# Seven of eleven pairs of the first SwiGLU products by seven products, with a pair's weights by quarters through the shared rings

## The chip, the cores and the metric

The kernel runs on one core of one Trainium2 chip. The metric is device time in microseconds (us) of one execution; before the change the median of three runs is 2079.83 us (2079.77 to 2080.1). Engines are named as in the profile: PE (TensorE matmul; PEld are its weight loads), DVE (VectorE), ACT (ScalarE), POOL (GpSimd), SP (SyncE, which issues most loads).

## The reference, cut to what matters

Two layers; each is a half-step SwiGLU, a mixer, and a second half-step SwiGLU, each followed by a residual sum and a layer norm. `x` is 512 positions by 1024 features, all in float32; `D_FF` is 2816, so `w13` is 1024 by 5632.

```python
def swiglu(x, w13, w2):
    a, b = jnp.split(x @ w13, 2, axis=-1)
    return (jax.nn.silu(a) * b) @ w2

for l in range(DEPTH):
    x = layer_norm(ALPHA * x + 0.5 * swiglu(x, ffn1_w13[l], ffn1_w2[l]), ln_g[l, 0], ln_b[l, 0])
    m = mixer(x, ...)
    x = layer_norm(ALPHA * x + m, ln_g[l, 1], ln_b[l, 1])
    x = layer_norm(ALPHA * x + 0.5 * swiglu(x, ffn2_w13[l], ffn2_w2[l]), ln_g[l, 2], ln_b[l, 2])
```

So there are four SwiGLU stages in a run, and the change is in the first product (`x @ w13`, then `silu(a) * b`) of each.

## The kernel before

Every float32 product is made of three products of `float32r` parts: an operand is split into a high part (ACT copies it with rounding, `split`, L119) and a low part (DVE subtracts, L122), and hi*hi, hi*lo and lo*hi are summed in PSUM. A split of a 128x1024 weight tile is one ACT and one DVE instruction.

The 5632 columns of `w13` are 22 blocks of 128 columns for `a` and 22 for `b`. Block k and block k+11 form a pair, k = 0 to 10. `ffn` works on the pairs in this order:

- `front`, pairs 8, 9, 10, the plain way: `plain` loads two weight blocks (`weights`, L124 to L133), makes 2 x 24 matmuls of 512 columns per block (`proj`, L147) and ends with `glu`. Beside them DVE and ACT form the sums of `x` that the other way needs (`x_sums`).
- `by_seven`, pairs 0 to 5 (`S_PAIRS` is 6): the 2 x 2 block product (features halved, positions halved; weight rows halved, `a` and `b` columns) by a Winograd form with seven products instead of eight. `seven_pair` issues seven products of 24 matmuls of 256 columns into four PSUM banks A, B, C, E (L548), and ACT and DVE take them out (L557 to L572).
- `behind`, pairs 6 and 7, the plain way again, while DVE forms the sums of the activations for the second product (`activation_sums`, L314 to L341), for all pairs from 10 and 0 onward.
- Then `Seven.run`, the second product (L363).

For one pair `weights_of_pair` loads four quarters of its weights (each 128 partitions x 2 blocks x 512), forms three further sums on DVE, and splits seven operands. Names before: `r_p` (two tiles, each an `a` quarter of the upper rows beside a `b` quarter of the lower rows), `rc` (`a`, lower rows), `rd` (`b`, upper rows); the sums are `t13` (two tiles, L521), `t2` (L522) and `rc + t2` (L526).

Buffers: a ring `raw` of 4 tiles for loaded weights (`NRAW`), a ring `w` of 10 tiles for split parts (`NW`, five operands of hi and lo), a ring `rs` of 2, a ring `sa` of 3, and 33 slots (`NS`) for everything that lives longer. Before, a pair takes two of `raw` (`r_p`), both of `rs` (`rc`, `rd`) and three slots (`t13` twice, `t2`); the first pair's `rc` and `rd` lie in slots and are loaded early (`raw_cd(..., True)`). A loaded tile's next use waits until its last reader is through: the load on SP waits for that instruction, and the queue of SP waits behind it.

Who sets the order: the code is written in the order above, and a scheduler of the framework moves instructions of an engine past each other by its own estimates when the program is built; what stands on an engine after that is fixed and runs in order. Beside the stage POOL issues DMAs that add up weight sums of the second product in DRAM (`sums_in_dram`, L288), a chain in which each step waits for the one before.

Of the kernel before, what the change touches and what calls it, by code (L numbers as in the profile page):

```python
# [35 lines left out]
P = 128  # L36
# [47 lines left out]
def trunk(ctx: ExitStack, tc, x_in, xt_in, w13, w2, w_in, w_br, w_out, ln_g, ln_b, lb_in, hgn, sgg, sgb, sgws,  # L84
# [18 lines left out]
    def slot(name, dtype=F32):  # L103
        return big.tile([P, 2, 512], dtype, tag="h", name=name, bufs=NS)
# [382 lines left out]
            s[c] = hi, lo  # L487
        return s

    def raw_cd(w13_of, k, early=False):  # L490

        if early:
            rc, rd = slot(f"rc{k}"), slot(f"rd{k}")
        else:
            rc, rd = (wk.tile([P, 2, 512], F32, tag="rs", name=f"r{c}{k}", bufs=2) for c in "cd")
        for z, j in enumerate((k, k + NH2)):
            nc.sync.dma_start(rd[:, z], w13_of(NF + j)[:, H[0]])
            nc.sync.dma_start(rc[:, z], w13_of(j)[:, H[1]])
        return rc, rd

    def weights_of_pair(w13_of, k, rcd=None):

        js = (k, k + NH2)
        ra = [wk.tile([P, 2, 512], F32, tag="raw", name=f"r_p{j}", bufs=NRAW) for j in js]
        rc, rd = rcd or raw_cd(w13_of, k)
        t13 = [slot(f"t13{j}") for j in js]
        t2 = slot(f"t2{k}")
        for z, j in enumerate(js):
            wa, wb = w13_of(j), w13_of(NF + j)
            nc.sync.dma_start(ra[z][:, 0], wa[:, H[0]])  # L510
            nc.sync.dma_start(ra[z][:, 1], wb[:, H[1]])

        def parts(raw, name, early=False):
            hi, lo = ((slot(f"{v}_{name}", F32R) if early else
                       wk.tile([P, 2, 512], F32R, tag="w", name=f"{v}_{name}", bufs=NW)) for v in "hl")
            split(hi, lo, raw, early)
            return [(hi[:, z], lo[:, z]) for z in range(2)]

        p = [parts(ra[z], f"p{j}") for z, j in enumerate(js)]
        for z in range(2):  # L520
            V.tensor_tensor(t13[z], ra[z], rd[:, z:z + 1].broadcast_to([P, 2, 512]), op=ALU.add)  # L521
            V.tensor_tensor(t2[:, z], ra[z][:, 0], t13[z][:, 1], op=ALU.add)  # L522
        w2 = parts(t2, f"t2{k}")
        wt = [parts(t13[z], f"t{j}") for z, j in enumerate(js)]
        w21 = parts(rc, f"c{k}", True)
        V.tensor_tensor(rc, rc, t2, op=ALU.add)  # L526
        w4 = parts(rc, f"d{k}", True)
        return p, wt, w2, w21, w4

    def seven_pair(seven, s, k, w):  # L530

        p, wt, w2, w21, w4 = w
        half = slice(0, 256), slice(256, 512)
        movs = {"A11": lambda m: (xh[m // 2][:, m % 2, half[0]], xl[m // 2][:, m % 2, half[0]]),
                "A12": lambda m: (xh[2 + m // 2][:, m % 2, half[0]], xl[2 + m // 2][:, m % 2, half[0]]),
                "A22": lambda m: (xh[2 + m // 2][:, m % 2, half[1]], xl[2 + m // 2][:, m % 2, half[1]])}
        for c in s:
            movs[c] = lambda m, c=c: (s[c][0][:, m], s[c][1][:, m])

        def product(ps, units, c, first=True):  # L540
            for z in range(2):
                hi, lo = units[z]
                for m in range(4):
                    ms = slice(m * P, (m + 1) * P)
                    mh, ml = movs[c](m)
                    for i, (a, v) in enumerate(((hi, mh), (hi, ml), (lo, mh))):
                        start = first and z == 0 and m == 0 and i == 0
                        PE.matmul(ps[:, half[z]], a[:, ms], v, start=start, stop=(m == 3 and i == 2),  # L548
                                  skip_group_check=not (first and z == 0))
                    flow.tick(3 * 120.0)  # L550

        A, B, C, E = (bank(f"f{c}{k}") for c in "ABCE")
        r = seven.room(k).rearrange("p q t -> p (q t)")
        lower, upper = r[:, 0:512], r[:, 512:1024]
        b0, b1 = (wk.tile([P, T], F32, tag="sa", name=f"b{c}", bufs=NSA) for c in "01")
        product(A, [p[0][0], p[1][0]], "A11")
        S.activation(upper, A, AF.Copy)  # L557
        product(B, w2, "s2")
        V.tensor_tensor(upper, upper, B, op=ALU.subtract)
        product(C, [wt[0][0], wt[1][0]], "s1")  # L560
        V.tensor_tensor(b1, C, upper, op=ALU.subtract)
        product(E, [wt[0][1], wt[1][1]], "s3")
        V.tensor_tensor(b1, b1, E, op=ALU.subtract)
        product(A, w21, "A12", False)
        S.activation(lower, A, AF.Silu)
        product(C, [p[0][1], p[1][1]], "s4", False)
        V.tensor_tensor(b0, C, upper, op=ALU.subtract)
        V.tensor_tensor(lower, lower, b0, op=ALU.mult)
        product(E, w4, "A22", False)
        V.tensor_tensor(upper, E, upper, op=ALU.add)  # L570
        S.activation(upper, upper, AF.Silu)
        V.tensor_tensor(upper, upper, b1, op=ALU.mult)  # L572

    S_PAIRS = 6

    def ffn(l, i, last=False, first_of_all=False):
        seven = Seven(lambda k: w2[l, i, k])
        w13_of = lambda j: w13[l, i, j]

        def blocks(j, early=False):  # L580
            return (weights(w13_of(j), f"a{j}", early), weights(w13_of(NF + j), f"b{j}", early),
                    bank(f"pa{j}"), bank(f"pb{j}"))

        def pair_of(j, args, n0, n):
            wa, wb, pa, pb = args
            proj(pa, wa, 0, from_x, KT, n0, n)
            proj(pb, wb, 0, from_x, KT, n0, n)

        def glu(j, args):
            wa, wb, pa, pb = args  # L590
            k, a = j % NH2, j // NH2
            sa = wk.tile([P, T], F32, tag="sa", name="sa", bufs=NSA)
            S.activation(sa, pa, AF.Silu)
            V.tensor_tensor(seven.part(k, a), sa.rearrange("p (h t) -> p h t", h=2),
                            pb.rearrange("p (h t) -> p h t", h=2), op=ALU.mult)

        front = list(range(Seven.KEPT, NH2))
        by_seven = list(range(S_PAIRS))
        behind = list(range(S_PAIRS, Seven.KEPT))
        sums = iter(range(NH2))  # L600

        def plain(j, args=None):
            args = args or blocks(j)
            pair_of(j, args, 0, T)
            glu(j, args)


        js = [j for k in front for j in (k, k + NH2)]
        if first_of_all:
            begin_features()  # L610
            wa = load_wx(w13_of(js[0]))
            for q in range(1, 4):
                load_xt(q)
            plain(js[0], (wa, weights(w13_of(NF + js[0]), "b0"), bank("pa0"), bank("pb0")))
            seven.weight_sums(next(sums))
            plain(js[1])
        else:
            first = [blocks(j, True) for j in js[:2]]
            need(0, 1)
            for z, j in enumerate(js[:2]):  # L620
                pair_of(j, first[z], 0, 256)
            need(2, 3)
            for z, j in enumerate(js[:2]):
                pair_of(j, first[z], 256, 256)
                glu(j, first[z])
                if z == 0:
                    seven.weight_sums(next(sums))
        seven.activation_sums(front[0])
        seven.weight_sums(next(sums))
        for z, j in enumerate(js[2:]):  # L630
            args = blocks(j)
            if z == 3:
                w = weights_of_pair(w13_of, by_seven[0], rcd)
            plain(j, args)
            if z == 0:
                s = x_sums()
            if z == 1:
                rcd = raw_cd(w13_of, by_seven[0], True)
            if z == 0:
                seven.weight_sums(next(sums))  # L640
            if z == 1:
                seven.activation_sums(front[1])
        in_dram = flow.add(seven.sums_in_dram(list(sums)))
        for k in by_seven:
            seven_pair(seven, s, k, w if k == by_seven[0] else weights_of_pair(w13_of, k))
        due = [front[2:] + by_seven[:2], by_seven[2:5], by_seven[5:] + behind[:1], behind[1:]]
        for z, j in enumerate([j for k in behind for j in (k, k + NH2)]):
            plain(j)
            for k in due[z]:
                seven.activation_sums(k)  # L650
        flow.finish(in_dram)
        seven.run(0.5 / ALPHA, (l, 2 * i), last)
# [480 lines left out]
```

## Time and profile before

| what | value |
|---|---|
| median of three runs | 2079.83 us |
| the profiled execution | 2079.87 us, of it 2078.1 us span |
| PE busy | 2058.0 us (99%) |
| DVE busy | 1465.7 us (71%) |
| ACT busy | 869.9 us (42%) |
| POOL busy | 284.8 us (14%) |
| granted TensorE clock | 0.999 |
| HBM read, written | 344.66 MB, 101.71 MB |

Times in the views are microseconds from the span's start. In a row of the timeline stand start, duration, engine, line, operation, tile written and tiles read, and in brackets how long the engine stood idle before it and for what. A duration holds the instruction's whole way through its engine, so that neighbours overlap; the distance from start to start is what one more instruction costs in a full queue. For matmuls the ends are modelled.

The four stages by seven products run from 76.16 to 197.11, from 765.35 to 886.31, from 1108.02 to 1228.97 and from 1798.60 to 1919.55.

### The profile page before, as it was taken

The numbers are of one execution on the slowest core, as the hardware profiler recorded it, in microseconds if no ns is written. First come the engines' busy times: TensorE is split into PE (matmuls) and PEld (weight loads), VectorE is DVE, ScalarE is ACT, GpSimd is POOL, SyncE is SP. The second block draws the span as 40 slices with busy tenths as digits, with TensorE's granted clock in tenths as the row PEclk, the third lists the DMA queues.
The fourth block names the chain that finished last, engine by engine and source line by source line (L and its number), as shares of the span: only waits on it lengthen the run. The fifth ranks groups of instructions, "written<-read, shape, count | busy, mean of one in ns | idle before, by whom it ended". The sixth has DMA issues, their size and how long they took to land.

```text
span 2078.1 us, 30349 instructions
## 1 busy us (share of the span) xinstructions
PE 2058.0 (99%) x11752; PEld 1810.8 (87%) x11752; DVE 1465.7 (71%) x2283; ACT 869.9 (42%) x1218; POOL 284.8 (14%) x424
## 2 busy tenths in 40 slices
PE   8999999999999999999999999999999999999998
PEld 6999888888888989988799998888888888899886
DVE  6887878943535788777778878779444357987776
ACT  4443555234322434445534446542343224444453
POOL 1222002001000212210112220020010002122001
PEclk9999999999999999999999999999999999999999
DMA  8788687122243578867768886861222426788674
GB/s 301 224 231 208 192 271 248 42 81 82 82 157 97 205 221 217 207 174 277 234 218 241 218 209 199 276 211 52 82 87 87 143 97 232 222 207 224 178 259 146
DMA packets 142273, 381.27 MB, mean 183 GB/s; under 512 B 16560, under 2 KB 16816, under 8 KB 142128
## 3 DMA queue, kind: packets, MB, share of 16 engines
q1 hardware_dynamic: 99792, 258.13, 37.6%
q0 software_dynamic: 42336, 121.20, 22.5%
q8 instruction: 92, 1.51, 0.3%
q14 instruction: 53, 0.43, 0.1%
HBM read 344.66 MB, written 101.71 MB: 215 GB/s over the span
## 4 chain that ended last, share of the span: by engine, by line
PE 95%; DMA 2%; DVE 1%; ACT 1%; issue 0%; POOL 0%; SPq 0%; POOLq 0%; DVEq 0%; ACTq 0%
PE pb L147 10%; PE pa L147 10%; PE z L147 8%; PE fE L548 7%; PE fC L548 7%; PE fA L548 7%; PE pA L363 5%; PE pC L363 5%; PE y L229 4%; PE y L147 4%; PE fB L548 3%; PE pB L363 3%; PE pF L363 2%; PE q L147 2%; PE pE L363 2%; PE f L147 2%
## 5 line engine op out<-in xcount | busy, mean ns | idle before, releaser
L147 PE MATMUL pa<-xh,h_a 128*128 128x512 f32 (+1 forms) x368 | 134.6, 366 | 6.5 <-ACT xh L119 6.2
L122 DVE TENSOR_TENSOR l_b<-r_b,h_b 128x1024 fp32r<-128x1024 f32 x84 | 102.3, 1222 | 54.5 <-ACT h_b L119 53.9
L288 POOL DMA_DIRECT2D t<-in_w_dram x128 | 106.4, 888 | 218.0 <-DMA t<-in_w_dram 103.1
L147 PE MATMUL pa<-xl,h_a 128*128 128x512 f32 (+1 forms) x368 | 134.6, 366 | 0.9 <-DVE xl L122 0.9
L147 PE MATMUL pb<-xh,h_b 128*128 128x512 f32 (+1 forms) x368 | 133.5, 363 | 0.2 <-ACT h_b L119 0.2
L147 PE MATMUL pb<-xh,l_b 128*128 128x512 f32 (+1 forms) x368 | 133.1, 362 | 0.5 <-DVE l_b L122 0.5
L147 PE MATMUL pa<-xh,l_a 128*128 128x512 f32 (+1 forms) x368 | 133.5, 363 | 0.0
L147 PE MATMUL pb<-xl,h_b 128*128 128x512 f32 (+1 forms) x368 | 133.0, 361 | 0.0
L119 ACT ACTIVATE h_b<-r_b 128x1024 fp32r<-128x1024 f32 x84 | 88.8, 1057 | 91.2 <-PE pa L147 33.3
L122 DVE TENSOR_TENSOR l_t<-t,h_t 128x1024 fp32r<-128x1024 f32 x72 | 87.3, 1222 | 42.3 <-ACT h_t L119 42.3
L119 ACT ACTIVATE h_t<-t 128x1024 fp32r<-128x1024 f32 x72 | 75.4, 1058 | 67.5 <-DVE t L522 48.7
L147 PE MATMUL z<-xh,h_z 128*128 128x512 f32 x256 | 102.6, 401 | 0.0
L147 PE MATMUL z<-xh,l_z 128*128 128x512 f32 x256 | 99.8, 390 | 0.0
L147 PE MATMUL z<-xl,h_z 128*128 128x512 f32 x256 | 99.8, 390 | 0.0
L122 DVE TENSOR_TENSOR l_z<-r_z,h_z 128x1024 fp32r<-128x1024 f32 x32 | 39.2, 1225 | 72.5 <-ACT h_z L119 72.4
L147 PEld LDWEIGHTS pa<-xh,h_a 128*128 128x128 f32 x368 | 69.7, 189 | 18.4 <-ACT xh L119 8.1
L147 PEld LDWEIGHTS pa<-xl,h_a 128*128 128x128 f32 x368 | 69.7, 189 | 13.6 <-DVE xl L122 3.2
L147 PEld LDWEIGHTS pb<-xh,l_b 128*128 128x128 f32 x368 | 69.4, 189 | 11.6 <-DVE l_b L122 1.0
L119 ACT ACTIVATE h_p<-r_p 128x1024 fp32r<-128x1024 f32 x48 | 50.4, 1057 | 69.5 <-PE fE L548 45.6
L147 PEld LDWEIGHTS pb<-xh,h_b 128*128 128x128 f32 x368 | 69.4, 189 | 11.1 <-ACT h_b L119 0.6
L147 PEld LDWEIGHTS pa<-xh,l_a 128*128 128x128 f32 x368 | 69.8, 190 | 10.5
L147 PEld LDWEIGHTS pb<-xl,h_b 128*128 128x128 f32 x368 | 69.4, 189 | 10.5
(348 smaller groups left out, 6675.4 us busy)
## 6 DMA issues: line engine op xcount, KB each, us to landing
t<-in_w_dram POOLq DMA_DIRECT2D x64, 512.0 KB, 9.1
r_p<-in_w_dram SPq DMA_DIRECT2D x96, 256.0 KB, 7.2
r_c<-in_w_dram SPq DMA_DIRECT2D x44, 512.0 KB, 5.6
r_d<-t SPq DMA_DIRECT2D x88, 256.0 KB, 4.2
r_b<-in_w_dram SPq DMA_DIRECT2D x40, 512.0 KB, 5.5
r_a<-in_w_dram SPq DMA_DIRECT2D x39, 512.0 KB, 5.3
t<-t POOLq DMA_DIRECT2D x76, 256.0 KB, 4.2
t<-in_w_dram POOLq DMA_DIRECT2D x64, 256.0 KB, 5.7
```

The source lines that it names most:

```text
L119: act = S.activation(hi, src, AF.Copy)
L122: V.tensor_tensor(lo, src, hi.bitcast(F32), op=ALU.subtract)
L147: PE.matmul(ps[:, n0:n0 + n], a[:, cs], m[:, n0:n0 + n], start=(i == 0), stop=(i == 3 * nk - 1))
L229: PE.matmul(ys[t][q], a[:, ts], m[:, q * 512:(q + 1) * 512], start=(k == 0 and i == 0), stop=(k == nk - 1 and i == 2))
L288: tc.keep_in_program_order(nc.gpsimd.dma_start(*of(k), **kw))
L363: PE.matmul(ps[tt], a[:, ts], m, start=(start and k == 0 and z == 0), stop=(stop and k == NH2 - 1 and z == 2), skip_group_check=not start)
L548: PE.matmul(ps[:, half[z]], a[:, ms], v, start=start, stop=(m == 3 and i == 2), skip_group_check=not (first and z == 0))
```

## The change

`S_PAIRS` goes from 6 to 7, so `by_seven` is pairs 0 to 6 and `behind` is pair 7 alone. `weights_of_pair` is written anew: four tiles of a pair, each holding one quarter for both blocks: `ra` (`a`, upper rows), `rb` (`b`, upper rows), `rd` (`b`, lower rows) in ring `raw`, and `rc` (`a`, lower rows) in ring `rs`, whose other tile is `rt`, a sum. Sums are made in place, four DVE instructions of 128x1024 (L504, L505, L506, L511). No slot is used and nothing is loaded early for the first pair. Each of the seven operands holds both blocks and is used by exactly one product. The sums of the activations of the last front pair and of pairs 0 to 2 are made within the stage by seven products, those of the others during pair 7.

```diff
@@ in ffn's helpers
-    def raw_cd(w13_of, k, early=False):
-        if early:
-            rc, rd = slot(f"rc{k}"), slot(f"rd{k}")
-        else:
-            rc, rd = (wk.tile([P, 2, 512], F32, tag="rs", name=f"r{c}{k}", bufs=2) for c in "cd")
-        for z, j in enumerate((k, k + NH2)):
-            nc.sync.dma_start(rd[:, z], w13_of(NF + j)[:, H[0]])
-            nc.sync.dma_start(rc[:, z], w13_of(j)[:, H[1]])
-        return rc, rd
-
-    def weights_of_pair(w13_of, k, rcd=None):
...
+    def weights_of_pair(w13_of, k):
+
+        a, b, d = (wk.tile([P, 2, 512], F32, tag="raw", name=f"r{c}_{k}", bufs=NRAW) for c in "abd")
+        t3, c = (wk.tile([P, 2, 512], F32, tag="rs", name=f"r{c}_{k}", bufs=2) for c in "tc")
+        for raw, col, row in ((a, 0, 0), (b, NF, 0), (d, NF, 1), (c, 0, 1)):
+            for z, j in enumerate((k, k + NH2)):
+                nc.sync.dma_start(raw[:, z], w13_of(col + j)[:, H[row]])
+
+        def parts(raw, name):
+            hi, lo = (wk.tile([P, 2, 512], F32R, tag="w", name=f"{v}_{name}{k}", bufs=NW) for v in "hl")
+            split(hi, lo, raw, name != "B11")
+            return hi, lo
+
+        w = {1: parts(a, "B11")}
+        V.tensor_tensor(t3, d, b, op=ALU.add)
+        V.tensor_tensor(b, a, b, op=ALU.add)
+        V.tensor_tensor(a, a, t3, op=ALU.add)
+        w[6] = parts(a, "t2")
+        w[5] = parts(b, "t1")
+        w[7] = parts(t3, "t3")
+        w[2] = parts(c, "B21")
+        V.tensor_tensor(c, a, c, op=ALU.add)
+        w[3] = parts(d, "B22")
+        w[4] = parts(c, "t4")
+        return w
 
     def seven_pair(seven, s, k, w):
 
-        p, wt, w2, w21, w4 = w
...
         def product(ps, units, c, first=True):
             for z in range(2):
-                hi, lo = units[z]
+                hi, lo = units[0][:, z], units[1][:, z]
...
-        product(A, [p[0][0], p[1][0]], "A11")
+        product(A, w[1], "A11")
         S.activation(upper, A, AF.Copy)
-        product(B, w2, "s2")
+        product(B, w[6], "s2")
...
-    S_PAIRS = 6
+    S_PAIRS = 7
@@ in ffn
             if z == 3:
-                w = weights_of_pair(w13_of, by_seven[0], rcd)
+                w = weights_of_pair(w13_of, by_seven[0])
             plain(j, args)
             if z == 0:
                 s = x_sums()
-            if z == 1:
-                rcd = raw_cd(w13_of, by_seven[0], True)
...
         for k in by_seven:
             seven_pair(seven, s, k, w if k == by_seven[0] else weights_of_pair(w13_of, k))
-        due = [front[2:] + by_seven[:2], by_seven[2:5], by_seven[5:] + behind[:1], behind[1:]]
+            if k <= 3:
+                seven.activation_sums(front[2] if k == 0 else by_seven[k - 1])
+        due = [by_seven[3:6], by_seven[6:] + behind]
```

The order in which the seven products are made stays: B11 (`w[1]`), t2, t1, t3, B21, B22, t4.

What the program makes of it, at the two places that matter for the weights of a pair. First DVE in the first SwiGLU stage, before, from the last sum of pair 1's weights (`rc1`) to the third operand of pair 2 (`r_p2` and `r_p13` are pair 2's loaded tiles, `r1` and `b1` are where pair 1's products are taken out of the banks `fB1`, `fC1`, `fE1`):

```order
L526 TENSOR_TENSOR rc1_902<-rc1_902,t21_910 128x1024
L122 TENSOR_TENSOR l_d1_945<-rc1_902,h_d1_944 128x1024
L559 TENSOR_TENSOR r1_952<-r1_952,fB1_949 128x512
L122 TENSOR_TENSOR l_p2_1155<-r_p2_1139,h_p2_1154 128x1024
L521 TENSOR_TENSOR t132_1147<-r_p2_1139,rd2_1142 128x1024
L561 TENSOR_TENSOR b1_954<-fC1_950,r1_952 128x512
L522 TENSOR_TENSOR t22_1149<-r_p2_1139,t132_1147 128x512
L521 TENSOR_TENSOR t1313_1148<-r_p13_1140,rd2_1142 128x1024
L563 TENSOR_TENSOR b1_954<-b1_954,fE1_951 128x512
L122 TENSOR_TENSOR l_p13_1159<-r_p13_1140,h_p13_1158 128x1024
L522 TENSOR_TENSOR t22_1149<-r_p13_1140,t1313_1148 128x512
L122 TENSOR_TENSOR l_t22_1167<-t22_1149,h_t22_1166 128x1024
```

Here the sum that reads the loaded `rd2` stands four instructions behind pair 1's last sum. Now the same stretch of DVE after the change (`tl0` belongs to the activation sums of pair 0):

```order
L511 TENSOR_TENSOR rc_1_916<-ra_1_912,rc_1_916 128x1024
L122 TENSOR_TENSOR l_B221_950<-rd_1_914,h_B221_949 128x1024
L544 TENSOR_TENSOR r1_961<-r1_961,fB1_958 128x512
L122 TENSOR_TENSOR l_t41_954<-rc_1_916,h_t41_953 128x1024
L122 TENSOR_TENSOR tl0_1150<-r0_708,th0_1149 128x256
L546 TENSOR_TENSOR b1_963<-fC1_959,r1_961 128x512
L504 TENSOR_TENSOR rt_2_1162<-rd_2_1161,rb_2_1160 128x1024
L122 TENSOR_TENSOR l_B112_1173<-ra_2_1159,h_B112_1172 128x1024
L548 TENSOR_TENSOR b1_963<-b1_963,fE1_960 128x512
L505 TENSOR_TENSOR rb_2_1160<-ra_2_1159,rb_2_1160 128x1024
L506 TENSOR_TENSOR ra_2_1159<-ra_2_1159,rt_2_1162 128x1024
L122 TENSOR_TENSOR l_t22_1180<-ra_2_1159,h_t22_1179 128x1024
```

The sum `rt_2`, which reads the loaded `rd_2`, now stands five instructions behind the last reader of `ra_1` (L511, first row). Second the queue of SP, before, around the loads of pairs 2 and 3:

```order
L510 DMA r_p3_1378<-in_w13_dram 128x512
L511 DMA r_p3_1378<-in_w13_dram 128x512
L497 DMA rd2_1142<-in_w13_dram 128x512 x2
L510 DMA r_p14_1379<-in_w13_dram 128x512
L511 DMA r_p14_1379<-in_w13_dram 128x512
L498 DMA rc2_1141<-in_w13_dram 128x512 x2
```

Each tile's two loads stand by themselves, and `rd` comes ahead of `rc`. After the change:

```order
L496 DMA rc_2_1163<-in_w13_dram 128x512 x2
L496 DMA rd_2_1161<-in_w13_dram 128x512 x2
L496 DMA ra_3_1405<-in_w13_dram 128x512 x2
L496 DMA rb_3_1406<-in_w13_dram 128x512 x2
L496 DMA rc_3_1409<-in_w13_dram 128x512 x2
L496 DMA rd_3_1407<-in_w13_dram 128x512 x2
```

All eight loads of a pair now stand in the order a, b, c, d. In the built program they wait as follows: before, `rd2` takes the buffer of `rd1` and waits for the second L521 of pair 1; after, `rd_2` takes the buffer of `ra_1` and waits for L511 of pair 1, `rc_2` takes the buffer of `rt_1` and waits for the split of t3 of pair 1, `ra_3` takes that of `rd_1` and waits for the split of B22 of pair 1, and `rb_3` that of `rb_2`, waiting for the split of t1 of pair 2. The loads of pair 5's `rd` wait for the split of B22 of pair 4, since the two last readers stand in the other order there. This pattern is the same in all four stages.

More of the change, by code (lines that the diff above doesn't have):

```diff
@@ L488, in x_sums @@
         return s
-    def raw_cd(w13_of, k, early=False):
-        if early:
-            rc, rd = slot(f"rc{k}"), slot(f"rd{k}")
-        else:
-            rc, rd = (wk.tile([P, 2, 512], F32, tag="rs", name=f"r{c}{k}", bufs=2) for c in "cd")
-        for z, j in enumerate((k, k + NH2)):
-            nc.sync.dma_start(rd[:, z], w13_of(NF + j)[:, H[0]])
-            nc.sync.dma_start(rc[:, z], w13_of(j)[:, H[1]])
-        return rc, rd
-    def weights_of_pair(w13_of, k, rcd=None):
[L503 to L528, printed above, removed]
@@ L555, in seven_pair @@
         b0, b1 = (wk.tile([P, T], F32, tag="sa", name=f"b{c}", bufs=NSA) for c in "01")
-        product(A, [p[0][0], p[1][0]], "A11")
+        product(A, w[1], "A11")
         S.activation(upper, A, AF.Copy)
-        product(B, w2, "s2")
+        product(B, w[6], "s2")
         V.tensor_tensor(upper, upper, B, op=ALU.subtract)
-        product(C, [wt[0][0], wt[1][0]], "s1")
+        product(C, w[5], "s1")
         V.tensor_tensor(b1, C, upper, op=ALU.subtract)
-        product(E, [wt[0][1], wt[1][1]], "s3")
+        product(E, w[7], "s3")
         V.tensor_tensor(b1, b1, E, op=ALU.subtract)
-        product(A, w21, "A12", False)
+        product(A, w[2], "A12", False)
         S.activation(lower, A, AF.Silu)
-        product(C, [p[0][1], p[1][1]], "s4", False)
+        product(C, w[3], "s4", False)
         V.tensor_tensor(b0, C, upper, op=ALU.subtract)
         V.tensor_tensor(lower, lower, b0, op=ALU.mult)
-        product(E, w4, "A22", False)
+        product(E, w[4], "A22", False)
         V.tensor_tensor(upper, E, upper, op=ALU.add)
```

## The prediction

> **What bounds the kernel now.** I read the page's busy shares and chain first, then the four stages by seven products.
>
> ```profile
> span 2078.1 us, 30349 instructions
> PE 2058.0 (99%) x11752; PEld 1810.8 (87%) x11752; DVE 1465.7 (71%) x2283; ACT 869.9 (42%) x1218; POOL 284.8 (14%) x424
> PE 95%; DMA 2%; DVE 1%; ACT 1%; issue 0%; POOL 0%; SPq 0%; POOLq 0%; DVEq 0%; ACTq 0%
> core 0: us, PE busy (x) PEld busy (x) DVE busy (x) ACT busy (x) POOL busy (x), PEclk, DMA share, GB/s
> 76.16:197.11 120.95, 120.95 (x1009) 120.94 (x1008) 99.35 (x111) 53.80 (x60) 27.89 (x39) 1.00 0.86 216
> 197.11:240.66 43.55, 43.55 (x194) 36.06 (x193) 30.56 (x62) 17.07 (x30) 5.34 (x8) 1.00 0.60 168
> 765.35:886.31 120.96, 120.96 (x1010) 120.95 (x1009) 99.35 (x111) 53.79 (x60) 28.23 (x39) 1.00 0.86 214
> ```
>
> PE is the bound: the chain is 95% PE. A stage by seven is six pairs in 120.95, 20.16 a pair, with PE never idle; the two plain pairs behind it take 43.55, 21.78 a pair. But DVE has 99.35 of 120.95 in the stage, 16.6 of each 20.16, and the DMA engines are 0.86 busy. So I look at what DVE waits for there, from pair 3 on (it starts at 136.64 on PE):
>
> ```profile
> 139.30 1.22 DVE L526 TENSOR_TENSOR rc<-rc,t 128x1024 f32<-128x1024 f32 x1
> 141.64 1.23 DVE L122 TENSOR_TENSOR l_d<-rc,h_d 128x1024 fp32r<-128x1024 f32 x1 [1.12 <-ACT h_d L119]
> 142.78 0.68 DVE L559 TENSOR_TENSOR r<-r,fB 128x512 f32<-128x512 f32 x1
> 143.38 1.22 DVE L521 TENSOR_TENSOR t<-r_p,rd 128x1024 f32<-128x1024 f32 x1
> 144.52 1.22 DVE L122 TENSOR_TENSOR l_p<-r_p,h_p 128x1024 fp32r<-128x1024 f32 x1
> ...
> 149.72 0.68 DVE L522 TENSOR_TENSOR t<-r_p,t 128x512 f32<-128x512 f32 x1
> 151.62 1.23 DVE L122 TENSOR_TENSOR l_t<-t,h_t 128x1024 fp32r<-128x1024 f32 x1 [1.21 <-ACT h_t L119]
> ...
> 212.70 0.42 DVE L334 TENSOR_TENSOR r<-r,s 128x256 f32<-128x256 f32 x1
> 213.04 0.42 DVE L331 TENSOR_TENSOR s<-r,s 128x256 f32<-128x256 f32 x1
> ```
>
> Start to start, a 128x1024 instruction costs 1.14 ("long", 143.38 to 144.52), a 128x512 one 0.60 ("mid", 142.78 to 143.38), a 128x256 one 0.34 ("short", 212.70 to 213.04). Where a split follows its own sum, ACT's copy puts about 1.3 between them (149.72 to 151.62 less a mid). No wait for a load stands in these rows: DVE starts on pair 4's operands at 143.38, 13 us before PE begins that pair (156.80). Why loads are hidden shows in SP's rows of that stage:
>
> ```profile
> 127.94 0.80 SPq L497 DMA_DIRECT2D rd<-in_w_dram  x2
> 142.90 0.80 SPq L498 DMA_DIRECT2D rc<-in_w_dram  x2
> ```
>
> `rd` is issued at 127.94 and read at 143.38, 15.4 later. The times from issue to landing of one such load, first of `rd`, then of `rc` (eight each in the first stage), are far shorter:
>
> ```profile
> DMA to landing us min/median/max: 5.5/6.6/9.7
> ...
> DMA to landing us min/median/max: 2.7/6.0/10.3
> ```
>
> **The change, part by part.**
>
> *One plain pair less, one by seven more.* 96 matmuls of 512 columns (21.78) become 168 of 256 (20.16): 1.62 a stage, 6.5 over four, all on PE's path. On the Trainium skill's page "TensorE: Matmul & The Clock Gate", section "Back-to-back issue gap", the isolated gap is N/2.4 + 2.5 ns, 216 and 109 ns; an estimate from that is 9.7 over four. The rows say 227 and 120 ns (43.55 over 192 matmuls, 120.95 over 1008), and I go by them.
>
> *DVE's work for a pair.* Before: 2 long and 2 mid and 1 long for sums, 7 long for splits, 7 mid to take out products; now 4, 7 and 7: the same 16.7. ACT and the number and size of loads (8 of 256 KB) stay too. Cost nothing.
>
> *Activation sums moved into the stage.* One of them is 4 short (L330 to L334) and the splits, 1 short and 1 mid: 2.3. Four now stand among DVE's work of pairs 0 to 4, so such a pair needs 19.0 of 20.16: still covered by PE, but the cover is 1.1. Five (11.5) remain beside the last plain pair, in 21.78 of which the old ones used 15.3 (half of 30.56): hidden there. POOL's two stores of the last front pair's pieces now stand earlier among its DRAM sums; those feed the second product, more than a pair later: nothing.
>
> *The slots that `t13`, `t2`, `rc0`, `rd0` leave, and products that use one operand each:* a gain only if PE waited for operands; it does not. Nothing.
>
> *The load of `rd`.* This is the term that decides. Three tiles of a pair share a ring of four, so only `ra` is loaded a pair ahead. `rd` of pair k+1 starts when L511 of pair k is through, and L504 of pair k+1, which reads it, stands four to six instructions later on DVE, with everything of pair k+1 behind it. The price is a loop that runs from L511 to L511 and has to fit into 20.16. In the loop: L511 itself 1.22, two semaphores 0.2, the load. No row has a load that is waited for here, so I bound it: 2.7 (shortest `rc`) to 10.3 (longest). I take 7.0: the median of `rd`, 6.6, because it too is issued just behind another load, and 0.4 since L504 needs both of two loads (0.80 for two issues). So 8.4 from L511's start to L504's. Then DVE's own rows to the next L511, counted in the order of the built program, with 1.3 for ACT behind L506:
>
> - pair 0 to 1: 8 long, 7 mid, 4 short: 16.0, loop 24.4
> - 1 to 2: 8 long, 6 mid, 5 short: 15.7, loop 24.1
> - 2 to 3 and 3 to 4: 7 long, 6 mid, 4 short: 14.2, loop 22.6 each
> - 4 to 5 (no activation sums left): 7 long, 4 mid: 11.7, loop 20.1
>
> Together 113.8 where PE needs five pairs, 100.8: DVE falls 13.0 behind. What lead does it have? PE's second product of pair 6 wants the split of t2 at 20.16 + 2.88 = 23.0 after pair 5 starts; from L511 of pair 5 that split is through after 8.4 + 4 long + 1 mid + 1.3 + 1.25 = 16.1, so L511 may start 6.9 into its pair. It starts, in pair 0, at about that already. The first pair's `rd` is issued where `rc` of pair 1 stood before, behind the split of the last front weights:
>
> ```profile
> 66.44 1.43 SPq L498 DMA_DIRECT2D rc<-in_w_dram  x1
> rc<-in_w_dram SPq DMA_DIRECT2D x1, 256.0 KB, 7.9
> ...
> 754.76 1.14 SPq L498 DMA_DIRECT2D rc<-in_w_dram  x1
> rc<-in_w_dram SPq DMA_DIRECT2D x1, 256.0 KB, 10.5
> ```
>
> It lands at 74.3 in the first stage. L504, L505, L506, ACT and the split then end at 74.4 + 3.4 + 1.3 + 1.25 = 80.4, where PE wants it at 79.04: 1.4 lost. In the second stage 765.3 gives 771.4 against 768.23: 3.2 lost. I take 2.3 for each. L511 follows 10.0 after the landing, 6.7 into the (late) pair: the lead is 0.2. A stage loses 2.3 + 13.0 - 0.2 = 15.1, four lose 60.4.
>
> **Sum**, against the profiled execution (2079.87 with the 1.8 around its span; the median, 2079.83, is the same): 2079.9 - 6.5 + 60.4 = 2133.8; I say 2133. Each us of load more or less moves a stage by 6 (five loops and the last limit): at 6.0 the loss is 9 a stage, 2110; at 7.8, 20 a stage, 2153.
>
> **The rivals.**
>
> 1. *The load is hidden after all.* At a load of 4 us from the first issue all loops but the first two fit (21.4, 21.1, 19.6, 19.6, 17.1), and those two take 2.2 of a lead that is then 3: only the 6.5 shows, less 0.5 or so where a stage starts, 2073 to 2075. The turning point is near 5: there the loops lose up to 1 a stage and the start as much, which uses up the 1.62. For it: the shortest `rc` lands in 2.7, and a stretched stage leaves the queues emptier. Against: the medians of both, 6.0 and 6.6, and a DMA share of 0.86. The Trainium skill, "DMA: Bandwidth & Descriptors", section "Anatomy of one DMA", gives 2.0 us + bytes/436 GB/s, 2.6 us for 256 KB, which would make this the outcome. The trace does not agree: 6.0 and 6.6 are medians beside POOL's DRAM sums.
>
> 2. *Some of both.* The load is long only while POOL moves its 512 KB pieces; short loads in between let DVE catch up, as far as PE's pace allows, and about 1 to 3 a stage remain: 2077 to 2086, no clear change. Against: a late DVE catches up only in a loop under 20.16, which takes a load under 2.7 (16.0 + 1.4) to 4.5 (14.2 + 1.4) as long as there are activation sums.
>
> 3. *The queue gets worse.* `rd` is issued 2 to 3 us behind `rc` and both now run in PE's critical time. With 9 us for a load a stage loses 27: 2181. For it: 9.7 and 10.3 as longest. Against: the same loads in the same number, spread over a longer stage.
>
> 4. *DVE, not the load, is the bound:* if the activation sums alone were too much, 19.0 + 1.3 + small waits would be about 20.5 against 20.16, 1 to 2 a stage: 2080. Its rows have the room; chance with rival 2.
>
> **How the numbers follow.** What a measurement of this kernel tells from no change is about 0.2%, 4 us. Forecast, a load of 6 to 8 us and 2090 to 2160: 0.79. Rival 1: 0.09, faster. Rivals 2 and 4: 0.07, of it 0.04 within 0.2%, 0.01 faster and 0.02 slower. Rival 3: 0.05. So faster 0.10, same 0.04, slower 0.86. The range 2090 to 2160 leaves out rival 1, most of 2, and 3, about 0.2 in all.
>
> **What the profile after would show.** Right: in the stages by seven DVE idle ahead of L504, released by the load of `rd`, 2 to 4 us six times a stage; PE idle ahead of the second or fourth product of a pair (banks B, E), released by DVE's splits of t2 or t3, some 15 a stage; the seven pairs in about 156 instead of 141.1; `rd` landing in 6.5 to 7.5; the plain pair at 21.8 and the second product unchanged. Wrong: L504 without idle time and PE at 20.16 a pair (rival 1), `rd` at 9 (rival 3), or DVE without gaps and yet late (rival 4). An idle PE at the start of the second product or ahead of pair 7 would be something that I have not seen.

## The result: 3.6% slower, and the profile after

The changed kernel takes 2156.46 us (median of five, 2151.55 to 2160.49) against 2079.83 (five, 2078.31 to 2080.89): a ratio of 1.0364 [1.0352, 1.0376], 76.6 us more. The forecast was 2133, in a range of 2090 to 2160. The profiled execution's span is 2156.0, 77.9 longer than before.

First the page's head:

```profile
span 2156.0 us, 31153 instructions
PE 2077.9 (96%) x12040; PEld 1839.5 (85%) x12040; DVE 1509.1 (70%) x2307; ACT 878.2 (41%) x1234; POOL 284.9 (13%) x424
```

Then the four stages by seven products, with two of the plain pairs behind them (columns as in the prediction: length, busy time of each engine, granted clock, DMA share, GB/s):

```profile
76.73:237.49 160.76, 147.20 (x1178) 145.72 (x1177) 131.65 (x153) 66.72 (x81) 33.30 (x47) 0.97 0.78 202
237.49:259.27 21.78, 21.78 (x98) 18.02 (x97) 16.00 (x31) 9.18 (x16) 0.00 (x0) 1.00 0.28 97
786.09:949.09 163.00, 146.72 (x1178) 145.24 (x1177) 131.17 (x153) 66.70 (x81) 33.26 (x46) 0.97 0.77 198
949.09:970.87 21.78, 21.78 (x98) 18.02 (x97) 16.01 (x31) 9.18 (x16) 0.00 (x0) 1.00 0.30 97
1146.82:1306.61 159.79, 146.58 (x1177) 145.10 (x1176) 131.21 (x153) 66.71 (x81) 34.11 (x47) 0.97 0.79 203
1855.87:2019.24 163.37, 149.33 (x1178) 148.01 (x1177) 130.78 (x152) 66.71 (x81) 33.40 (x47) 0.95 0.77 198
```

Seven pairs at 20.16 would be 141.1. The stages take 159.8 to 163.4, and PE, which never stood idle there before, now does; it is also busy for longer (146.6 to 149.3), at a granted clock of 0.95 to 0.97. To part the two, I took the starts of all matmuls of these stages: where one starts over 0.5 behind the one before, the distance beyond 0.12 is idle time, and what the other distances have beyond 0.12 is slowness. Idle: 14.7, 17.4, 14.3, 15.0, together 61.4. Slow: 5.0, 4.5, 4.3, 7.3, together 21.0. So the account is 61.4 + 21.0 - 6.5 (the saving) = 75.9; the other 2.0 of the span's 77.9 lie in the second products (108.74, 107.33 and 108.99 for 106.71, 109.54 and 106.79; the fourth is 104.63 in both).

What PE waits for, over the whole run (columns: waiting engine, tile and line, what ended the wait, us, times, longest):

```profile
PE fE L533 <- DVE b L548: 41.2, 15, 4.4
PE fC L533 <- DVE b L546: 8.2, 4, 3.2
PE pa L147 <- ACT xh L119: 6.4, 2, 5.3
PE fB L533 <- ACT h_t L119: 4.7, 4, 1.5
PE fB L533 <- DVE l_t L122: 3.0, 4, 0.8
```

Only the last two are where the prediction looked, at the second product, and they are the start of each stage. Most of the time PE waits ahead of the *seventh* product (and in pair 0 ahead of the sixth) for bank E (or C), until DVE has taken the earlier product out of it. DVE's rows around one such wait (pair 3 of the first stage) say why; the rows of SP and PE are of the same stretch:

```profile
154.59 1.23 DVE L511 TENSOR_TENSOR rc<-ra,rc 128x1024 f32<-128x1024 f32 x1
155.74 1.22 DVE L122 TENSOR_TENSOR l_B<-rd,h_B 128x1024 fp32r<-128x1024 f32 x1
156.87 0.68 DVE L544 TENSOR_TENSOR r<-r,fB 128x512 f32<-128x512 f32 x1
157.47 1.22 DVE L122 TENSOR_TENSOR l_t<-rc,h_t 128x1024 fp32r<-128x1024 f32 x1
158.60 0.68 DVE L546 TENSOR_TENSOR b<-fC,r 128x512 f32<-128x512 f32 x1
159.21 0.42 DVE L122 TENSOR_TENSOR tl<-r,th 128x256 fp32r<-128x256 f32 x1
159.54 1.22 DVE L122 TENSOR_TENSOR l_B<-ra,h_B 128x1024 fp32r<-128x1024 f32 x1
164.27 1.23 DVE L504 TENSOR_TENSOR rt<-rd,rb 128x1024 f32<-128x1024 f32 x1 [3.52 <-DMA rd<-in_w_dram]
165.41 0.68 DVE L548 TENSOR_TENSOR b<-b,fE 128x512 f32<-128x512 f32 x1
...
155.84 1.03 SPq L496 DMA_DIRECT2D rd<-in_w_dram  x2
...
166.24 0.36 PE L533 MATMUL fE<-xh,h_t 128*128 128x256 f32 x1 [3.71 <-DVE b L548]
```

L511 ends, SP issues `rd` of pair 4 the moment after, and L504, which needs it, starts 9.7 after L511. L548 stands behind L504: it has nothing to do with `rd`, but DVE works in order. Its bank is what PE needs. Over all stages DVE stood idle ahead of L504 as follows (the four under `ra` are the first pairs of the stages; `issue` means that the profile names no releaser, and those four stand from pair 1 to 2 and from pair 5 to 6 in the first two stages, where in the other two stages the load of `rd` ends the wait):

```profile
its engine sat idle before it (us, times) until:
  DMA rd<-in_w_dram: 54.6, 17
  DMA ra<-in_w_dram: 30.0, 4
  issue: 17.9, 4
  DVE b L548: 0.7, 1
```

The loads of `rd` themselves, from issue to landing:

```profile
rd<-in_w_dram SPq DMA_DIRECT2D x56, 256.0 KB, 6.7
```

And the clock around that wait, in four pieces: the end of the sixth product, the wait, the 3.9 us behind it, and the next 3.4:

```profile
162.00:162.50 0.50, 0.50 (x5) 0.33 (x3) 0.00 (x0) 0.00 (x0) 0.00 (x0) 1.00 0.97 332
162.50:166.20 3.70, 0.03 (x1) 0.00 (x0) 1.93 (x3) 0.00 (x0) 1.05 (x1) 1.00 1.01 184
166.20:170.10 3.90, 3.86 (x20) 3.89 (x21) 2.68 (x3) 1.52 (x2) 0.56 (x1) 0.56 1.00 174
170.20:173.60 3.40, 3.40 (x31) 3.40 (x30) 3.40 (x7) 1.52 (x4) 1.40 (x2) 1.00 0.40 130
```

Behind the wait PE has a granted clock of 0.56 and starts 20 matmuls in 3.9 us; then it is back at 1.00, and starts 31 in 3.4.

### The profile page after: what moved, and what is told of

The parts are those of the page before. It is cut to its first block, busy times and chain, and to the rows that moved or that the text cites. A ratio compares the mean times of both kernels' runs of the same rounds, so it can differ in the third digit from the quotient of the medians.

```text
span 2156.0 us, 31153 instructions
## 1 busy us (share of the span) xinstructions
PE 2077.9 (96%) x12040; PEld 1839.5 (85%) x12040; DVE 1509.1 (70%) x2307; ACT 878.2 (41%) x1234; POOL 284.9 (13%) x424
## 5 line engine op out<-in xcount | busy, mean ns | idle before, releaser
L533 PE MATMUL fA<-xh,h_B 128*128 128x256 f32 x448 | 127.2, 284 | 0.0
L533 PE MATMUL fA<-xl,h_B 128*128 128x256 f32 x448 | 127.0, 283 | 0.0
L533 PE MATMUL fA<-xh,l_B 128*128 128x256 f32 x448 | 127.0, 283 | 0.0
L119 ACT ACTIVATE h_t<-ra 128x1024 fp32r<-128x1024 f32 x28 | 29.6, 1058 | 203.6 <-DVE ra L506 203.6
L533 PE MATMUL fE<-xh,h_t 128*128 128x256 f32 x224 | 72.4, 323 | 41.2 <-DVE b L548 41.2
L147 PE MATMUL pb<-xh,h_b 128*128 128x512 f32 (+1 forms) x304 | 108.5, 357 | 0.0
L504 DVE TENSOR_TENSOR rt<-rd,rb 128x1024 f32<-128x1024 f32 x28 | 34.3, 1225 | 103.3 <-DMA rd<-in_w_dram 54.6
L533 PEld LDWEIGHTS fE<-xh,h_t 128*128 128x128 f32 x224 | 50.4, 225 | 44.0 <-issue 44.0
L533 PEld LDWEIGHTS fA<-xh,h_B 128*128 128x128 f32 x448 | 86.7, 194 | 0.2
L533 PEld LDWEIGHTS fA<-xl,h_B 128*128 128x128 f32 x448 | 86.4, 193 | 0.2
```

Of the source, the lines that this page charges most:

```text
L119: act = S.activation(hi, src, AF.Copy)
L147: PE.matmul(ps[:, n0:n0 + n], a[:, cs], m[:, n0:n0 + n], start=(i == 0), stop=(i == 3 * nk - 1))
L504: V.tensor_tensor(t3, d, b, op=ALU.add)
```

## The experiments

Three questions: is it the load of `rd` (the ring), or DVE's own work, or the seventh pair? What does the place of L548 add? What does a wait cost PE beside the time that it stands idle? Idle and slow time are counted as above.

**Six tiles in the ring.**

```diff
-    NS, NRAW, NSA = 33, 4, 3
+    NS, NRAW, NSA = 31, 6, 3
```

> The changed kernel with six tiles in the ring raw instead of four (two slots fewer pay for them), so that rd of a pair waits for the split of B22 two pairs earlier and not for L511 of the pair before. Load-loop theory: L504 no longer waits for rd, DVE's evictions are no longer held up behind it, PE loses at most the start of a stage: seven pairs in 141 to 143 us, 2073 to 2083, point 2075. Rival, DVE's own work with the activation sums is the bound: the same DVE work remains, stages of 143 or more with PE waiting for DVE that is never idle, 2085 to 2110. Rival, the order on DVE (sums of the next pair ahead of evictions) costs by itself, load or no load: waits at the banks C and E remain, above 2100.

Measured: 2068.33 (2067.94 to 2069.19), 0.9948 [0.9936, 0.996] of the kernel before, faster than both. The first stage:

```profile
76.25:217.36 141.11, 141.11 (x1178) 141.11 (x1176) 125.54 (x147) 65.35 (x78) 33.17 (x46) 1.00 0.86 225
```

And what DVE waits for ahead of L504 now, no load any more:

```profile
  PE fC L533: 7.0, 12
```

All four stages are 141.11 long with no gap on PE, with the same instructions for a pair (2307 on DVE in both kernels), the same activation sums and the same order a, b, c, d of loads. The order on DVE alone does not cost it: from pair to pair of the first stage L548 stands behind L504 five times of six here, as often as in the changed kernel, and PE never waits for it. It is the ring. The rest of the gain beyond 6.5 lies outside these stages: in the profiles the second products are 2.8 shorter than before (106.75 for 109.54 in the second stage), the fronts 1.5, nearly all of it ahead of the fourth stage. These differ from run to run, and I did not follow them.

**Five tiles.** The same edit with 32 and 5.

> The changed kernel with five tiles in the ring raw and one slot fewer. rd of a pair then waits for the split of t1 of the pair before, about 10 us ahead of L511. Load-loop theory: that is lead enough for a load of 7, no waits at L504, the same as six tiles: 2064 to 2073, point 2068. Rival, a whole pair of lead is needed because loads in this stage sometimes take 10: some waits of 1 to 3 us remain, 2075 to 2095.

Measured: 2071.17 (2068.81 to 2072.29), 0.9956 [0.9941, 0.9971]. Again 141.11 in every stage. One more tile is enough, since it lets `rd` start behind the split of t1 of the pair before (for pair 2 of the first stage it is issued at 94.78 and read at 105.38).

**The new weights of a pair with six pairs.**

```diff
-    S_PAIRS = 7
+    S_PAIRS = 6
-        due = [by_seven[3:6], by_seven[6:] + behind]
+        due = [by_seven[3:5], by_seven[5:], behind[:1], behind[1:]]
```

> The changed kernel with six pairs by seven instead of seven: the new weights of a pair alone, without the seventh pair. Load-loop theory: no saving of 6.5, and the loss of the changed kernel less that of the boundary from pair 5 to 6 (about 4 us of idle PE and 2 of slow clock in each stage): 2125 to 2145, point 2137. Rival, the seventh pair and the activation sums that it pulls into the stage are what costs: 2080 to 2090.

Measured: 2136.12 (2130.05 to 2137.81), 1.0268 [1.0251, 1.0284]. In the stages 37.0 idle and 13.8 slow: the loss comes without the seventh pair.

**The seventh pair with the old weights.** In the kernel before; its weights of a pair hold slots, which the activation sums need too, so all nine sums stand behind the stage:

```diff
-    S_PAIRS = 6
+    S_PAIRS = 7
-        due = [front[2:] + by_seven[:2], by_seven[2:5], by_seven[5:] + behind[:1], behind[1:]]
+        due = [front[2:] + by_seven[:4], by_seven[4:] + behind]
```

> The kernel before with seven pairs by seven and its own weights of a pair (slots, rd and rc loaded a pair ahead): the seventh pair alone. There are no free slots for activation sums within the stage, so all nine stand beside the one plain pair. Theory, the change loses by its rings and not by the seventh pair: 6.5 less than before, 2073, up to 2080 if the nine sums (20.7 of DVE's time beside 21.8 of PE) reach into the second product. Rival, the seventh pair itself costs: 2090 or more.

Measured: 2083.01 (2081.77 to 2085.66), 1.0018 [1.0009, 1.0027]: outside of what I expected, by the way that I had named. First stage and second product of this kernel:

```profile
77.06:218.17 141.11, 141.11 (x1178) 141.11 (x1176) 116.32 (x130) 62.70 (x70) 31.98 (x44) 1.00 0.85 212
239.96:350.44 110.48, 107.95 (x480) 87.80 (x479) 93.32 (x137) 64.81 (x88) 12.48 (x20) 1.00 0.74 253
```

Two of PE's waits in the second products:

```profile
PE pB L363 <- ACT h_t L119: 5.2, 4, 1.4
PE pB L363 <- DVE l_t L122: 1.4, 4, 0.4
```

The stages save their 1.62 each (141.11 and 21.79), and the second products give back more: 437.1 for 428.1 in sum, since nine sums of activations beside one plain pair reach into them (DVE is busy for 93.32 in the first, with 137 instructions; before, 84.53 with 115). So the place of the sums in the stage is worth 9 us. That they can stand there only with the freed slots is read from the code; no run puts them there with the old weights.

**The eviction first.** L504 is pinned behind L548 of the pair before, and nothing else.

```diff
-        V.tensor_tensor(t3, d, b, op=ALU.add)
+        with ExitStack() as st:
+            if ev:
+                st.enter_context(tc.issue_after(ev.pop()))
+            V.tensor_tensor(t3, d, b, op=ALU.add)
...
-        V.tensor_tensor(b1, b1, E, op=ALU.subtract)
+        ev[:] = [V.tensor_tensor(b1, b1, E, op=ALU.subtract).ins]
```

> The changed kernel with one order pinned on DVE: L504 of pair k+1 stands behind the instruction that takes bank E of pair k out (L548), no longer ahead of it. In the changed kernel PE waits 41 us of 57 for that eviction, which stands behind the waiting L504. Load-loop theory: the loop L511, load, L504 stays longer than 20.16, so DVE stays late and the wait moves to the split of t2 (second product, bank B) of the next pair; idle PE 30 to 55 us in all; the half-clock stretches shrink with the longest waits: 2110 to 2145, point 2130. Rival, the place of the eviction alone is what costs: its 41 to 49 us and the 25 us of slow clock go away, 2080 to 2092.

Measured: 2125.22 (2120.83 to 2126.86), 1.0214 [1.0198, 1.023], 31 us faster than the changed kernel. Idle 36.7, slow 18.9. PE's longest waits of this kernel, whose lines stand five further down:

```profile
PE fB L538 <- ACT h_t L119: 16.5, 10, 3.0
PE fB L538 <- DVE l_t L122: 15.2, 14, 1.7
```

The waits at bank E are gone, and those at the second product, where the prediction had put them all, are there instead. So of 61 us idle, 25 hung on an eviction that stood behind the waiting sum; 37 remain with the eviction first, and with the ring of five or six they go too.

**Less traffic.** POOL's accumulating transfers are left out.

```diff
-                    for of, kw in ((copy, {}), (add, {"accum_op": ALU.add})):
+                    for of, kw in ((copy, {}),):
```

> The changed kernel without the accumulating half of POOL's sums in DRAM (the second product's weight sums are then wrong; the plain copies stay), so that less traffic runs beside the loads of the pairs. Theory, the load's 7 us is what it takes beside POOL's transfers, and the loop loses 6 us a stage for each us: with a load of 5 to 6 the idle time falls from 61 to 15 to 40 us and the slow-clock part with it: 2090 to 2130, point 2110. Rival, the load's time does not come from POOL's transfers: 2145 to 2160.

Measured: 2102.52 (2099.06 to 2105.2), 1.0107 [1.0092, 1.0122]. Idle 20.6, slow 8.9. The loads of `rd`:

```profile
rd<-in_w_dram SPq DMA_DIRECT2D x56, 256.0 KB, 4.4
```

And PE's longest wait:

```profile
PE fE L533 <- DVE b L548: 11.4, 10, 3.5
```

The median load of `rd` falls from 6.7 to 4.4, and 40.8 of idle time go: 4.4 a stage for each us of load (6 in the prediction). The time of the load depends for a good part on the transfers beside it.

**Filling the wait.** 16 further matmuls ahead of the seventh product of pairs 3 and 5:

```diff
+        if k in (3, 5):
+            mh, ml = movs["s4"](3)
+            for i in range(16):
+                PE.matmul(B[:, half[0]], w[3][0][:, 1, 384:512], mh, start=(i == 0), stop=(i == 15), skip_group_check=True)
         product(E, w[4], "A22", False)
```

> The changed kernel with 16 extra matmuls of 256 columns (1.9 us at 0.12) between the sixth and the seventh product of pairs 3 and 5 of each stage, where PE waits 3 to 4.5 us for bank E; they write bank B, which nobody reads any more. Clock theory (after such a wait PE runs at half clock for up to 3.4 us, about 16 us in these eight places): the wait is split and shorter, the clock stays up, the work fits into the wait: 10 to 16 us faster than the changed kernel, 2140 to 2147. Rival, the slow matmuls behind a wait come from something that the fill does not touch (operands, weight loads): no change, 2152 to 2161, or slower by up to 15 us where the fill does not fit into the wait.

Measured: 2164.18 (2159.58 to 2167.83), 1.0407 [1.0388, 1.0425], some 8 us slower than the changed kernel. Idle 60.1, slow 18.8: it does not tell the two theories apart. The scheduler took the longer pair into account and set DVE's evictions of pairs 4 and 5 later, so new waits arose ahead of the sixth product (3.4 and 3.8 in the first stage). An edit that changes the order cannot show the price of a wait, so the next three make waits of a known length where there are none.

**Waits of a known length.** Five tiles in the ring (2071.17; one slot fewer still, for the scratch tile), and in each pair PE waits for copies on ACT:

```diff
+        def delay(n, bank):
+            g = wk.tile([P, 7, 256], F32R, tag="gap", name=f"gap{k}", bufs=1)
+            src = bank[:, 0:256].rearrange("p (o t) -> p o t", o=1)
+            for _ in range(n):
+                S.activation(g, src.broadcast_to([P, 7, 256]), AF.Copy)
+            tc.keep_in_program_order(PE.matmul(B[:, half[0]], w[1][0][:, 1, 384:512], g[:, 6], start=True, stop=True,
+                                               skip_group_check=True))
...
+        delay(2, C)
         product(E, w[4], "A22", False)
```

That is the first of them; the second has `delay(1, C)` ahead of the fourth and of the seventh product, the third a tile of `[P, 4, 256]` and `delay(1, A)` ahead of the second and of the sixth.

> To measure what a wait does to PE by itself: five tiles in the ring, and in every pair by seven (28 in all) PE waits once, between the sixth and the seventh product, for two copies on ACT (128x1792, about 1.9 us each, the second bank C into a scratch tile that only a dummy matmul into the free bank B reads): idle about 4.5 a pair, 126 us in all. Clock theory: after a wait of over 3.5 PE runs at half clock for some 16 matmuls, 1.5 to 2.5 us a pair more: 2230 to 2260, point 2245, and 40 to 60 above the same idle time cut in two. Rival, a wait costs its idle time and no more: 2190 to 2205, the same as cut in two.

> The same two copies on ACT and dummy matmuls, one ahead of the fourth and one ahead of the seventh product of every pair: two waits of about 2.2 us, some 126 us idle in all as well. Clock theory: waits of 2.2 are mostly too short to lower the clock: 2190 to 2215, point 2200. Rival, PE loses a fixed time at each restart, whatever the length of the wait: as much as or more than with one wait, 2230 or more.

> The measurement of waits again, with waits that are really short: five tiles in the ring, and in every pair by seven PE waits ahead of the second and of the sixth product for one copy of bank A on ACT (128x1024) behind the copy or Silu that takes A out: 56 waits of about 2.0, 112 us idle, and 7 us of dummy matmuls. Theory, a wait lowers the clock only from a length of about 2.3 to 3.7 on: nothing more than the idle time and 0.1 a wait, 2071 + 112 + 7 + 6 = 2196, 2180 to 2215. Rival, each restart costs about 1.5 whatever the length of the wait, as it did after waits of 3.8 and of 5.4: 2270 to 2290.

Measured: 2246.36 (2243.59 to 2249.64), 2359.3 (2357.0 to 2360.61) and 2227.43 (2226.69 to 2228.93). The first came out as expected, but the second shows that its waits were not what I meant them to be: 3.8 long instead of 2.2, because DVE's instruction on bank C came ahead of ACT's copy. In the third, one of the two is 1.8 and the other 2.7. That makes a scale of four lengths, here without the waits in the last pair of a stage, where matmuls of the plain pair fill them:

| wait | how many | slowness of over 0.5 behind it | slowness on average |
|---|---|---|---|
| 1.8 | 24 | 0 | 0.10 |
| 2.7 | 28 | 18 | 1.04 |
| 3.7 to 3.8 | 52 | 49 | 1.62 |
| 5.1 to 5.8 | 24 | 24 | 1.87 |

These give the times back: for the second kernel 52 x (3.79 + 1.62) and 56 dummy matmuls of 0.12 are 288.0, measured 288.1 over five tiles without waits; for the third 24 x 1.86 + 28 x 3.74 + 6.7 = 156.1, measured 156.3. The granted clock over a whole stage (the third number from the right), in the first kernel:

```profile
76.22:266.00 189.78, 158.87 (x1205) 156.39 (x1204) 127.21 (x147) 88.71 (x93) 33.14 (x46) 0.89 0.67 171
```

in the second:

```profile
76.60:293.50 216.90, 169.79 (x1207) 166.20 (x1206) 128.84 (x147) 88.03 (x92) 33.16 (x46) 0.89 0.59 150
```

and in the third:

```profile
76.74:259.40 182.66, 155.23 (x1199) 152.15 (x1198) 126.81 (x147) 78.55 (x92) 33.22 (x46) 0.95 0.69 177
```

So the forecast of the first kernel held, and the other two were for waits of 2.2 and 2.0 in every place, which these kernels do not make. Read by length, a wait of 1.8 costs itself and 0.1 more, one of 2.7 lowers the clock in two cases of three, one of 3.7 or longer nearly always; and once lowered, the price is 1.5 to 1.9, nearly the same for a wait of 3.8 and of 5.4. In the changed kernel all seven waits of over 3.5 were followed by slowness (2.2 on average), of the five from 2.3 to 3.4 one was, and of 15 under 2.2 one.

Where a wait lies counts as well as its length. In each of these traces the stretches at half clock are 3.41 or 6.83 long, apart from the last, which ends with the run, and all start on one grid of 3.41. Here are steps of that grid in the changed kernel, three at a wait of 3.3 in the second stage and two at the wait of 3.9 in the first:

```profile
801.46:804.87 3.41, 1.72 (x15) 1.52 (x13) 0.38 (x1) 0.00 (x0) 0.00 (x0) 1.00 0.84 300
804.87:808.28 3.41, 1.91 (x16) 1.91 (x17) 3.41 (x4) 0.00 (x0) 0.00 (x0) 1.00 0.01 4
808.28:811.69 3.41, 3.41 (x31) 3.41 (x30) 2.20 (x4) 1.26 (x2) 0.00 (x0) 1.00 0.00 0
163.17:166.58 3.41, 0.34 (x3) 0.37 (x4) 2.31 (x3) 0.00 (x0) 0.48 (x1) 1.00 1.00 175
166.58:169.99 3.41, 3.41 (x19) 3.41 (x18) 2.19 (x3) 1.41 (x2) 0.56 (x1) 0.50 1.01 175
```

The first wait is split over two steps, 1.7 and 1.5 idle, and the clock stays; the second leaves PE idle for 3.1 of one step, and the next step runs at half clock. In the stages of the eight kernels here with waits of over 1.5, all 114 full-clock steps with more than 2.05 idle were followed by half clock, none with less than 1.7, and 12 of the 40 in between. That accounts for the table: a wait of 1.8 hardly reaches the limit, one of 2.7 does or does not by where it falls, and one of 3.8 misses it only when it is split nearly in half. One step of 3.41 at half clock loses 1.7. It also names the one short wait that was followed by slowness: two, of 1.5 and 0.9, lay in the same step. What makes a second step of half clock follow the first is open; less idle time was enough there.

**Eight pairs by seven, six tiles.**

```diff
-    S_PAIRS = 7
+    S_PAIRS = 8
...
-            if k <= 3:
-                seven.activation_sums(front[2] if k == 0 else by_seven[k - 1])
+            seven.activation_sums(front[2] if k == 0 else by_seven[k - 1])
+        seven.activation_sums(by_seven[7])
```

> Six tiles in the ring, and eight of eleven pairs by seven: no plain pair behind the stage; the activation sums of the pair before stand in each pair, those of pair 7 behind the stage. If DVE's 16.7 + 2.3 = 19.0 a pair still fit under PE's 20.16 and the second product does not wait for pair 7's sums: 1.62 less in each stage than with seven pairs, 2062, 2059 to 2065. Rival, the last pair's evictions, its sums and their splits have no cover any more and PE waits 2 to 4 us ahead of or within the second product: 2068 to 2078.

Measured: 2067.59 (2066.26 to 2067.71), 0.9942 [0.9929, 0.9956]: no better than six tiles and seven pairs (0.9948 [0.9936, 0.996]), and between the two ranges that I had named. The stage is 162.51, against 141.11 + 21.79 = 162.90: 0.4 of the 1.62 is left. PE waits once in each stage, at bank A:

```profile
PE fA L533 <- ACT r L542: 3.9, 4, 1.0
```

## Why the prediction was right, and where its sum fell short

**Right: the loop.** The load of `rd` behind L511 is what makes the kernel slower. Four tiles against five or six, with one or two slots fewer and the rest alike, are worth 85 to 88 us; six pairs lose as well; DVE's own work (rival 4) is the same with six tiles, without any loss; the load is not hidden (rival 1), short loads do not catch up (rival 2), and it is not at 9 (rival 3). The formula that rival 1 takes from the Trainium skill ("DMA: Bandwidth & Descriptors", "Anatomy of one DMA") stands there for DMAs that GpSimd issues, and these loads are SP's; the measured 6.7 and 4.4 decide.

**Right in size: the load and the idle time.** From L511's start to L504's I took 8.4; in the trace it is 8.75 on average over 20 (6.7 to 11.7; without the four from pair 4 to 5, whose load does not wait for L511: 5.5 to 7.7), and the loads of `rd` land in 6.7 at the median. The five loops from L511 of pair 0 to L511 of pair 5, 113.8 in the prediction, are 110.8, 114.2, 111.0 and 114.6. In that sum two errors cancel: from pair 3 to 4 the loop is 24.5 to 25.1 and not 22.6, and from pair 4 to 5 17.4 to 19.6 and not 20.1, because the prediction let that load wait for L511 as well. Idle time was forecast at 60.4 and is 61.4. At the start of a stage I took 2.3; the waits at fB, 4.7 + 3.0 over four stages, are 1.9 each. The plain pair is at 21.78, and DVE's waits ahead of L504 are there, 1.1 to 7.0 us at five or six of the six boundaries of a stage.

**The term that failed: what a wait costs.** "A stage loses 2.3 + 13.0 - 0.2" counts idle time alone. The clock that follows the waits is missing: 21.0 over four stages, 5.3 a stage, nearly the whole distance from 2133 to 2156. It could not be read from the profile before, where PE never waits in these stages, but it was a cost to be bounded and I did not ask for it. That 2156 still lies in the range, 4 us below its upper end, is luck: the range was that wide for the time of the load, and the load came as expected. The Trainium skill's page that I had used for the spacing of matmuls, "TensorE: Matmul & The Clock Gate", says in its first part ("What's actually happening") that the clock falls to half after an idle window of about 3.4 us that runs free, and returns after a busy one. The runs agree in kind: 0.56 for 3.9 us behind a wait of 3.7, and stretches at half clock that keep to a grid of 3.41. They differ in the size: the window need not be idle as a whole, over 2.05 of its 3.41 were always enough. The section "Why this matters for your kernels" puts the bound at gaps of about 3 us; here 18 of 28 waits of 2.7 were punished.

**The place, wrong.** I had L548 in the order that I quoted, two rows behind L504 (which itself stands six instructions behind L511, not five), and named as the next late thing only the split of t2 for the second product of the next pair. PE needs bank E 6 x 2.88 = 17.3 into the pair; from L511 the loop needs 8.4, L504 1.14 and L548 with its semaphore some 0.8, or 1.1 more where the split of B11 stands between: L511 has to start by 7.0 or 5.8. My limit for t2 was 6.9. The two limits lie so close that the wrong one gave the right idle time, but not the same kernel: with L548 ahead of L504 25 us of idle time go, and only then do the waits stand where I had put them.

**Wrong in part: "nothing" for the freed slots.** In the kernel with the old weights and seven pairs the activation sums stand behind the stage, and the second products pay 9 us for it. If the slots are what lets them stand in the stage, as the code says, they are worth that.

**Sensitivity.** I put 6 a stage on each us of load; without the accumulating transfers it was 4.4. A likely reason, not shown by a run: waits that end at a bank, and loads of `rd` that land in 4.1 to 9.9, make an average of loops too sharp.

What stays open: the 2.0 in the second products after the change, the 4.3 by which six tiles gain outside of the stages, and how much of the price of the slots is due to them alone.

## What to carry to other kernels

When tiles are put on a shared ring, follow for each load which instruction frees its buffer and how far ahead of the first reader that is: a lead below the load's time under this traffic puts the load into the loop, however much the engines have to spare, and one more tile in the ring may be the whole cure. Then list everything behind the waiting reader on its in-order engine, and ask for each row when another engine needs it: an eviction of a PSUM bank is worth more than the sum that it stands behind. And price a wait of PE of 2 to 3.5 us at its length plus up to 1.8 us of slow clock, by where it falls, and a longer one at its length plus 1.4 to 2.8; two waits of under 2 are cheaper than one of 4, if they do not lie within the same 3.4 us.

## What the runs showed of the hardware that I had not expected

A wait of PE costs more than its length, by steps and not in proportion: 0.1 behind 1.8 us, 1.6 behind 3.8, 1.9 behind 5.4. The steps are those of a grid of 3.41 us: what counts is how long PE was idle within one of them, and the limit lies between 1.7 and 2.05. The same 256 KB load takes 6.7 at the median beside POOL's accumulating transfers and 4.4 with only the plain copies.
